# Attention with a bias: q and k of the last six pairs transposed by the DMA engines, and a new emission model

## The chip, the cores and the metric

The kernel runs on one core of a Trainium2 chip. The metric is device time in microseconds (us) of one execution. Before the change the median of 3 runs is 238.55 us (238.26 to 239.92). TensorE multiplies matrices (PE in the profile; PEld is its weight load), ScalarE evaluates functions (ACT), VectorE works elementwise (DVE), GpSimd (POOL) and SyncE (SP) here mostly issue DMAs. Each engine runs its own instructions in order; semaphores hold them until their inputs are there.

## The reference

Inputs: q, k and v of 4 batches x 8 heads x 1024 positions x 64, and one bias of 1024 x 1024 for all heads, float32.

```python
scale = 1.0 / np.sqrt(head_dim)
scores = scale * np.matmul(q, k.transpose(0, 1, 3, 2))
scores = scores + bias
scores_max = np.max(scores, axis=-1, keepdims=True)
attn = np.exp(scores - scores_max) / (np.sum(np.exp(scores - scores_max), axis=-1, keepdims=True) + 1e-8)
return np.matmul(attn, v).astype(np.float32)
```

## The kernel before

**Slots.** The 32 heads are 16 pairs, in groups of 4, 6 and 6 pairs (`GROUPS`). A query chunk has 128 rows, 8 chunks to a head. One chunk of one head is a slot, 256 in all. A slot is filled by 8 matmuls of 128x128x128 into one of three places in PSUM (`places`, of two banks each; `fill_half`, L221 and L224). Its 128x1024 scores are exponentiated into an `E` tile (`exp`, L238, on ScalarE; ring of 9), and 8 matmuls with V and a column of ones (`av`, L291) write 65 columns of a bank `po`. After 3 to 7 slots the bank is evicted by VectorE (`evac`, L299 reciprocal and L301 product) into one of two `ob` buffers, and SP stores it.

**Bias by difference.** A place's scores aren't cleared between heads: the bias is added by TensorE only at the first slot of a run (L221). After that each score matmul adds the next head's scores and takes off the ones before: `ko` and `qo` hold, on the 128 partitions, both heads of a pair (64 and 64), with the first head's q negated; `ke` and `qe` hold the first head of the pair and the second head of the pair before, negated. `qs` and `qz` hold one head with zeros beside it, for the starts.

**Preparation of a pair.** POOL loads k and q (L134, L142; `land` has 3 buffers each) and V, cast to bf16. VectorE lays the two heads side by side (`side_by_side`, L149, into `kr` and `qr`, two buffers each). TensorE transposes 128x128 blocks into a PSUM tile `px` (`transposes`, L178), which takes one of the two tags that the `po` banks also use. VectorE copies it out into `ko` (L185) or `qo` (L187, with the sign); and halves of these are doubled into `ke` (L196, or by an SP copy from pair 4 on, L495) and `qe`, `qs`, `qz` (L198, on VectorE or POOL). `kq` is a ring of 9 pairs.

**Slots on VectorE.** Some slots of the third place (19 in this version) are exponentiated by VectorE instead of ScalarE, in six steps on 128x1024 (`d_steps`: L255 dy, L260 df, L264 dt, L267 df, L270 dt, L275 de). L255 frees the PSUM place; the rest can wait.

**Order.** After a written-out prologue, a planner in the kernel's source (from T0 on) emits the order of each engine's instructions. It holds costs in ns, dates at which loads land (`land_at`, `v_at`, `bias_at`) and dates at which arrays are `ready`, and picks the next piece of work: for VectorE by `dve_pick` (earliest start, then a priority), for SP by date from `sp_q`. A slot goes to VectorE when `may_d` allows it and `backlog` is under `ROOM`. The planner's dates order the program; what an engine waits for on the chip is set by the semaphores alone.

Of the kernel before, what the change touches and what calls it, by code (L numbers as in the profile page):

```python
# [9 lines left out]
BF = mybir.dt.bfloat16  # L10
ACTF = mybir.ActivationFunctionType
ALU = mybir.AluOpType
# [4 lines left out]
def kernel(  # L17
# [13 lines left out]
    nc = tc.nc  # L31
    B, H, S, D = q.shape
    P = 128
# [10 lines left out]

    GROUPS = (4, 6, 6)
    RING = 9
    NE = 9
    C0 = 3

# [111 lines left out]
    def arrays(pr):  # L161
        if pr not in arrs:
            t = {x: kq.tile([P, NCH, P], BF, name=x) for x in (("ko", "ke", "qo", "qe") if pr else ("ko", "qo"))}
            if pr in split_pair:
                t["qs"] = qs
            if pr in first_pair:
                t["qz"] = qz[group_of[pr] % 2]
            arrs[pr] = t
        return arrs[pr]

    def linked(pr):
        return pr + 1 < NP

# [25 lines left out]
                            op0=ALU.mult, op1=ALU.mult)  # L199

    def parts(pr, which):
        return ([0] if pr else []) + ([1] if linked(pr) else []) + (
            [] if which else [2] * (pr in split_pair) + [3] * (pr in first_pair))

    def operands(s):
# [108 lines left out]
    with tc.manual_schedule():  # L314
# [60 lines left out]
        for c in range(5, NCH):  # L375
# [5 lines left out]
        EXP = 906  # L381
        ISSUE, COPY = 70, 4000
        T0 = 7400.0
        bias_at = {0: T0, 1: 8300, 2: 9700, 3: 20800, 4: 25600, 5: 30500, 6: 32000, 7: 33500}
        land_at = {(1, 1, 0): 11300, (1, 0, 0): 12100, (2, 1, 0): 15200, (2, 0, 0): 15800, (3, 1, 0): 18700,
                   (3, 0, 0): 19300, (0, 0, C0): 21700, (3, 0, C0): 24200, (1, 0, C0): 26600, (2, 0, C0): 27600}
        v_at, vland_at = {}, {0: 13600, 1: 17200, 2: 23200, 3: 29200}
        t_dma = 33500
# [6 lines left out]
        raw_at = {}  # L395

        q_items = [(p, 0, 0, C0) for p in range(1, GROUPS[0])] + [(p, 0, C0, NCH - C0) for p in (0, 3, 1, 2)]
        q_items += [(p, 0, 0, NCH) for p in range(GROUPS[0], NP)]
        k_items = [(p, 1, 0, NCH) for p in range(1, NP)]
        n1 = GROUPS[0] - 1  # L400
        pieces = [y for x in zip(k_items[:n1], q_items[:n1]) for y in x] + q_items[n1:n1 + GROUPS[0]]
        pieces += [y for x in zip(k_items[n1:], q_items[n1 + GROUPS[0]:]) for y in x]
# [11 lines left out]
        half_done = []  # L414
        waiting, free_lands, loads = [], set(), list(range(GROUPS[0], NP))
        sp_q, t_sp = [], T0
        AHEAD = 60
        DEP = 115
        ROOM = 5000
# [15 lines left out]
        def arrange(pr, which, c0, n):  # L435

            if (pr, which, c0) not in land_at:
                waiting.append((pr, which, c0, n))
                return
            urgent = need_at[pr, which, c0] - next_fill < 12  # L440
            cost = 90 + 40 * n

            def run(t2):
                side_by_side(pr, which, slice(c0, c0 + n))
                raw_at[pr, which, c0] = t2 + cost + L_DVE
                if which == 0 and c0 + n == NCH:
                    free_lands.add(pr)
                    while loads and loads[0] - 3 in free_lands:
                        load(loads.pop(0), t2)
            dve_q.append((land_at[pr, which, c0], 0 if urgent else 2, cost, run))  # L450

        def load(pr, t):
            load_k(pr)
            load_q(pr, slice(0, NCH))
            land_at[pr, 1, 0] = dma(pool(t, 750), 1800)
            land_at[pr, 0, 0] = dma(pool(t, 750), 1800)
            for p in [pr - 1] * (pr > GROUPS[0]) + [pr] * (pr + 1 == NP):
                load_v(p)
                v_at[p] = dma(pool(0, 1900), 4800)
            for x in [x for x in waiting if x[0] == pr]:  # L460
                waiting.remove(x)
                arrange(*x)

        def move_v(pr):
            def run(t2):
# [4 lines left out]
        def dma(at, cost):  # L470

            nonlocal t_dma
            t_dma = max(t_dma, at) + cost
            return t_dma + 2500

        def doubles(pr, which, c0, n, t2, urgent):
            for x in parts(pr, which):
                key = (("ke", "ke1")[x], pr + (x == 1)) if which else (("qe", "qe1", "qs", "qz")[x], pr + (x == 1), c0)
                if which and pr >= GROUPS[0]:
                    sp_q.append((t2 + L_DVE, lambda t3, x=x, key=key: copy_k(pr, x, key, t3)))  # L480
                elif which or urgent:
                    cost = 90 + 38 * n

                    def run(t3, x=x, key=key, cost=cost):
                        double(pr, which, c0, n, x, nc.vector)
                        ready[key] = t3 + cost + L_DVE
                    dve_q.append((t2, 0.2 if urgent else 2, cost, run))
                else:
                    double(pr, which, c0, n, x, nc.gpsimd)
                    pool(t2)  # L490
                    ready[key] = pool(0, 125 * n + 100) + 300
# [38 lines left out]
        def pe_cands():  # L530

            out = []
            for x in range(3):
                if not queue[x] or queue[x][0] > next_fill + WINDOW:
                    continue
                s = queue[x][0]
                r = fill_ready(s)
                if r is not None and (before[s] is None or before[s] in used):
                    cost = FILL * (2 if slots[s][3] else 1)

                    def do(t, s=s, x=x, cost=cost):
                        nonlocal next_fill
                        fill(s)
                        filled[s] = t + cost + L_PE
                        queue[x].pop(0)
                        next_fill = min([y[0] for y in queue.values() if y], default=NS)
                        if may_d[s] and backlog(t) < ROOM:
                            dslots.add(s)
                            avq.remove(s)
                            start_d(s)  # L550
                        else:
                            acts.append(s)
                    out.append((max(t_pe, r), cost, do, 0, s))
# [36 lines left out]
            if pieces:  # L590
# [39 lines left out]
        def pool(at, cost=0):  # L630
            nonlocal t_pool
            t_pool = max(t_pool, at) + cost
            return t_pool
# [8 lines left out]
                x_free[tag] = t2 + cost + L_DVE  # L642
            dve_q.append((t, 1, cost, run))

        chains, d_wait = [], []

        def backlog(t):
            x = max(0, t_dve - t) + sum(y[2] for y in dve_q if y[0] < t + 3000 and y[1] < 3)
            return x + sum(sum(y[0] for y in c) for c in chains) / 2 + sum(sum(y[0] for y in c[1:]) for r, s, c in d_wait) / 2

        def start_d(s):
            steps = d_steps(s)

            def first(t):
# [12 lines left out]
        def step(s, left, t):  # L667
            cost = left[0][0]

            def run(t2):  # L670
                left.pop(0)[1]()
                if left:
                    step(s, left, t2 + cost + DEP)
                    return
                dav.append((t2 + cost + L_DVE, s))
                chains[:] = [x for x in chains if x is not left]
                next_chain(t2 + cost)
            dve_q.append((t, 3, cost, run))

        def pe_pick():  # L680
            c = pe_cands()
# [13 lines left out]
            return min(ok + fills, key=lambda x: (x[0], x[3])) if ok + fills else None  # L695

        def dve_pick():
            if not dve_q:
# [12 lines left out]
        for x in k_items[:2] + q_items[:2]:  # L711
            arrange(*x)
        while next_fill < NS or next_act < len(acts) or avq or dav or dve_q or sp_q:
            c = []
# [65 lines left out]
```

## Time and profile before

| | value |
|---|---|
| median of 3 runs | 238.55 us |
| the profiled execution | 238.78 us |
| its span | 237.0 us |
| granted TensorE clock | 0.996 |
| DMA | 27.37 MB, mean 115 GB/s |
| exponentials on ScalarE | 236 full and 2 halves: 237 slots |
| slots on VectorE | 19 |

A row of the groups gives line, engine, operation, result and operands by name, shape, count, then busy us, mean ns of one, and idle us of the engine just before them with what ended it. Instructions overlap a little, so that a mean is longer than the step from one start to the next (an exponential takes 1084 ns on the mean, and ScalarE takes one each 0.92 us). A row of a timeline gives start, length, engine, line, operation, count and the gap ahead of it.

### The profile page before, as it was taken

The page shows a single profiled execution, that of the slowest core. Times are in us where ns is not written, and L with a number is a line of the kernel's source. Part 1 is how long each engine was busy: PE and PEld are TensorE (multiplying, and loading weights), DVE is VectorE, ACT ScalarE, POOL GpSimd, SP SyncE. Part 2 cuts the span into 40 slices and gives each one's busy share as a digit, 9 for nine tenths or more (in the row PEclk, how much of TensorE's full clock was granted, in tenths as well). Part 3 has the DMA queues.
Part 4 walks back from the last instruction along what each step waited for, and adds up shares of the span by engine and source line. Part 5 has one row for each costly group of instructions (what it writes and reads, how often), then busy time and mean ns, then how long its engine had stood idle before and what let it go on. Part 6 is the DMA issues. An engine that isn't in the chain of part 4 may idle for free.

```text
span 237.0 us, 10333 instructions
## 1 busy us (share of the span) xinstructions
PE 222.2 (94%) x4554; PEld 212.3 (90%) x4554; DVE 209.2 (88%) x335; ACT 222.0 (94%) x242; POOL 59.0 (25%) x80
## 2 busy tenths in 40 slices
PE   7779999999999999999999997999999999999883
PEld 2668999999999998999999996999999999999873
DVE  2668855799999989999999999999999999999981
ACT  3589999989999999999999999899999999999993
POOL 8828283710185414400000176000000000000000
PEclk9999999999999999999999999999999999999998
DMA  6999999992399999992111769133321111121112
GB/s 204 208 203 189 209 221 193 201 185 70 73 152 217 221 218 206 165 94 75 35 28 42 148 85 168 40 76 86 95 65 42 42 39 33 36 64 42 30 42 79
DMA packets 56140, 27.37 MB, mean 115 GB/s; under 512 B 32864, under 2 KB 53600, under 8 KB 56096
## 3 DMA queue, kind: packets, MB, share of 16 engines
q0 software_dynamic: 36304, 14.06, 50.2%
q1 hardware_dynamic: 19648, 12.13, 19.0%
q8 instruction: 35, 0.57, 1.0%
q10 hardware_dynamic: 144, 0.52, 0.7%
q14 instruction: 9, 0.07, 0.1%
HBM read 29.36 MB, written 8.39 MB: 159 GB/s over the span
## 4 chain that ended last, share of the span: by engine, by line
PE 54%; ACT 20%; DVE 15%; issue 7%; DMA 2%; SPq 0%; ACTq 0%; DVEq 0%
PE pl L224 30%; ACT E L238 20%; PE po L291 16%; PE px L178 5%; PE pl L221 4%; DVE ko L185 2%; DMA dt<-in_k_dram 2%; DVE qe L198 2%; DVE dt L270 1%; DVE qo L187 1%; DVE dt L264 1%; DVE ob L301 1%; DVE ke L196 1%; DVE dy L255 1%; DVE kr L149 1%
## 5 line engine op out<-in xcount | busy, mean ns | idle before, releaser
L238 ACT ACTIVATE E<-pl 128x1024 bf16<-128x1024 f32 (+1 forms) x238 | 218.8, 1084 | 6.6 <-PE pl L224 5.8
L291 PE MATMUL po<-vall,E 128*128 128x65 bf16 x1896 | 89.5, 194 | 1.5 <-issue 0.7
L224 PE MATMUL pl<-qo,ko 128*128 128x128 bf16 x1024 | 77.2, 219 | 4.0 <-ACT E L238 1.9
L224 PEld LDWEIGHTS <-ko 128*128 128x128 bf16 x1216 | 73.2, 98 | 7.0 <-issue 4.7
L291 PEld LDWEIGHTS <-E 128*128 128x128 bf16 x1896 | 76.5, 98 | 2.4 <-issue 1.2
L224 PE MATMUL pl<-qe,ke 128*128 128x128 bf16 x832 | 61.7, 219 | 2.5 <-DVE qe L198 1.2
L224 PEld LDWEIGHTS <-ke 128*128 128x128 bf16 x832 | 50.2, 98 | 4.8 <-issue 2.3
L134 POOL DMA_DIRECT2D k<-in_k_dram x15 | 11.2, 748 | 62.9 <-DVE kr L149 62.9
L255 DVE TENSOR_SCALAR dy<-pl 128x1024 int32<-128x1024 f32 x19 | 23.2, 1219 | 3.0 <-ACT E L238 2.6
L301 DVE TENSOR_TENSOR ob<-po,rs 128x384 f32<-128x384 f32 (+4 forms) x44 | 24.0, 546 | 1.5
L267 DVE SCALAR_TENSOR_TENSOR df<-dt,df 128x1024 f32<-128x1024 f32 x19 | 23.9, 1260 | 0.0
L275 DVE SCALAR_TENSOR_TENSOR de<-dy,dt 128x1024 uint16<-128x1024 int32 x19 | 23.3, 1229 | 0.0
L264 DVE SCALAR_TENSOR_TENSOR dt<-df 128x1024 f32<-128x1024 f32 x19 | 23.1, 1217 | 0.1
L270 DVE SCALAR_TENSOR_TENSOR dt<-df,dt 128x1024 f32<-128x1024 f32 x19 | 23.1, 1217 | 0.0
L159 POOL DMA_DIRECT2D vall<-in_v_dram x24 | 21.0, 878 | 0.4 <-issue 0.4
L142 POOL DMA_DIRECT2D q<-in_q_dram x18 | 13.0, 725 | 16.8 <-DVE qr L149 16.6
L221 PE MATMUL pl<-ident,braw 128*128 128x128 bf16 x192 | 16.1, 227 | 0.0
L187 DVE TENSOR_SCALAR qo<-px,sgn 128x1024 bf16<-128x1024 bf16 (+2 forms) x20 | 12.8, 639 | 2.4 <-PE px L178 2.4
L185 DVE COPY ko<-px 128x1024 bf16<-128x1024 bf16 (+1 forms) x17 | 11.1, 653 | 4.2 <-PE px L178 4.2
L198 DVE TENSOR_SCALAR qe<-qo 64x1024 bf16<-64x1024 bf16 (+2 forms) x35 | 13.8, 395 | 0.9
L299 DVE RECIPROCAL rs<-po 128x6 f32<-128x6 f32 (+4 forms) x44 | 8.4, 191 | 6.8 <-PE po L291 6.4
L221 PEld LDWEIGHTS <-braw 128*128 128x128 bf16 x192 | 14.0, 148 | 0.0
(48 smaller groups left out, 127.5 us busy)
## 6 DMA issues: line engine op xcount, KB each, us to landing
out_dram<-ob SPq DMA_DIRECT2D x52, 96.0 KB, 3.0
k<-in_k_dram POOLq DMA_DIRECT2D x15, 256.0 KB, 7.0
q<-in_q_dram POOLq DMA_DIRECT2D x12, 256.0 KB, 6.9
vall<-in_v_dram POOLq DMA_DIRECT2D x24, 128.0 KB, 7.1
ke<-ko SPq DMA_DIRECT2D x23, 128.0 KB, 4.7
out_dram<-ob SPq DMA_DIRECT2D x34, 64.0 KB, 1.9
braw<-in_bias_dram POOLq DMA_DIRECT2D x7, 256.0 KB, 6.9
v<-in_v_dram POOLq DMA_DIRECT2D x4, 256.0 KB, 6.4
```

Of the source, the lines that this page charges most:

```text
L159: nc.gpsimd.dma_start(out=vall[:, 2 * pr + t, :, :D], in_=vf[pr, :, t])
L198: w.tensor_scalar(to[("qe", "qe", "qs", "qz")[part]][rows, cs, :], t["qo"][rows, cs, :], -1.0, 1.0, op0=ALU.mult, op1=ALU.mult)
L221: nc.tensor.matmul(to, braw[:, c, :].rearrange("p (kp kc) -> p kc kp", kc=NCH)[:, kc, :], ident8[:], start=i == 0, stop=False, skip_group_ ...
L224: nc.tensor.matmul(to, kk[:, kc, :], qq[:, c, :], start=False, stop=True, skip_group_check=True)
L238: nc.scalar.activation(e[:, i:i + n].rearrange("p b x -> p (b x)"), places[slots[s][0]][:, i:i + n].rearrange("p b x -> p (b x)"), ACTF.Ex ...
L255: w.tensor_scalar(t["y"][:], places[slots[s][0]].rearrange("p b x -> p (b x)"), scale * LOG2E * 65536.0, 127.0 * 65536.0, op0=ALU.mult, op ...
L264: w.scalar_tensor_tensor(t["t"][:], t["f"][:], -G, t["f"][:], op0=ALU.add, op1=ALU.mult)
L267: w.scalar_tensor_tensor(t["f"][:], t["t"][:], Q, t["f"][:], op0=ALU.mult, op1=ALU.add)
L270: w.scalar_tensor_tensor(t["t"][:], t["f"][:], V, t["t"][:], op0=ALU.add, op1=ALU.mult)
L275: w.scalar_tensor_tensor(etile[s].bitcast(U16).rearrange("p c q -> p (c q)"), t["y"][:], 1.0 / 512.0, t["t"][:], op0=ALU.mult, op1=ALU.add)
L291: nc.tensor.matmul(po[:, j, :], etile[s][:, kc, :], vall[:, h, kc, :], start=j == 0 and kc == 0, stop=kc == NCH - 1, skip_group_check=True)
L301: nc.vector.tensor_tensor(ob[:, :n, :], po[:, :n, :D], rs[:, :n, :].to_broadcast([P, n, D]), op=ALU.mult)
```

## The change

`TURNED = 10`: pairs 10 to 15 (the last group) take another way from the loaded array to `ko`, `qo`, `ke` and `qe`. For k VectorE makes the same copy as before (L185 in the changed file); for q it makes four half copies (L186 to L189), which are two laid-out arrays: one with the first head negated (for `qo`), one with the second head of the pair before, negated (for `qe`). SP then issues DMAs that transpose the eight 128x128 blocks of each array straight into `ko`, `qo` and `qe` (L193): three for each pair, 18 in all. `ke` is copied on SP as before, `qz` (pair 10) and `qs` (pair 14) are copied on SP from `qe`. For these pairs TensorE's transposes, the copy-out and the doublings are gone, and so is the doubling from pair 9 into pair 10's `qe`.

The planner's dates and rules change too: bias, loads and V are booked earlier by 0.2 to 2.0 us; a doubling of its own pair comes ahead of the one for the next pair; at most three slots of VectorE may be open; their last step waits while two finished ones are in stock; ScalarE takes the smallest slot number among those already filled; TensorE transposes ahead of need only while fewer than four finished exponentials wait for their product with V, instead of six. The order that results holds 20 slots on VectorE.

```diff
+    TURNED = 10
...
+    def layout_steps(pr, which):
+        l = lands[pr, which]
+        t = {}
...
+        if which:
+            return [(410, lambda: nc.vector.tensor_copy(new(0).rearrange("p c t d -> p t c d"), l[:]))]
+        minus = lambda to, of: nc.vector.tensor_scalar(to, of, -1.0, None, op0=ALU.mult)
+        return [(HALF, lambda: minus(new(0)[:, :, 0, :], l[:, 0])),
+                (HALF, lambda: nc.vector.tensor_copy(t[0][:, :, 1, :], l[:, 1])),
+                (HALF, lambda: nc.vector.tensor_copy(new(1)[:, :, 0, :], l[:, 0])),
+                (HALF, lambda: minus(t[1][:, :, 1, :], lands[pr - 1, 0][:, 1]))]
+
+    def turn(to, of):
+        nc.sync.dma_start_transpose(to[:], of.rearrange("p c t d -> p c (t d)"))
...
     def parts(pr, which):
-        return ([0] if pr else []) + ([1] if linked(pr) else []) + (
+        return ([0] if pr else []) + ([1] if linked(pr) and (which or pr + 1 < TURNED) else []) + (
...
-        bias_at = {0: T0, 1: 8300, 2: 9700, 3: 20800, 4: 25600, 5: 30500, 6: 32000, 7: 33500}
+        bias_at = {0: T0, 1: max(T0, 8100), 2: 9300, 3: 19400, 4: 24000, 5: 28700, 6: 30300, 7: 31900}
...
-        q_items += [(p, 0, 0, NCH) for p in range(GROUPS[0], NP)]
-        k_items = [(p, 1, 0, NCH) for p in range(1, NP)]
+        q_items += [(p, 0, 0, NCH) for p in range(GROUPS[0], TURNED)]
+        k_items = [(p, 1, 0, NCH) for p in range(1, TURNED)]
...
+        def turning(to, of, t):
+            nonlocal t_turn, t_sp
+            turn(to, of)
+            t_sp += 1230
+            t_turn = max(t_turn, t) + 2700
+            return t_turn + 2200
+
+        def turn_k(pr, t):
+            done = turned[pr, 1] = ready["ko", pr] = turning(arrays(pr)["ko"], raws[pr, 1, 0], t)
+            for x in (0, 1)[:NP - pr]:
+                sp_q.append((done, lambda t2, x=x: copy_k(pr, x, (("ke", "ke1")[x], pr + x), t2)))
+
+        def turn_q(pr, t):
+            a = arrays(pr)
+            ready["qo", pr, 0] = turning(a["qo"], raws[pr, 0, 0], t)
+            done = turned[pr, 0] = ready["qe", pr, 0] = ready["qe1", pr, 0] = turning(a["qe"], raws[pr, 0, 1], t)
+            for x in ("qs", "qz"):
+                if x in a:
+                    def copy(t2, x=x):
+                        nc.sync.dma_start(out=a[x][:D], in_=a["qe"][:D])
+                        ready[x, pr, 0] = t2 + COPY
+                    sp_q.append((done, copy))
...
-            t_dma = max(t_dma, at) + cost
-            return t_dma + 2500
+            t_dma = max(t_dma + cost, at + 4700)
+            return t_dma + 200
...
-                    dve_q.append((t2, 0.2 if urgent else 2, cost, run))
+                    dve_q.append((t2, (0.2, 0.4, 0.4, 0.2)[x] if urgent else 2, cost, run))
...
-                        if may_d[s] and backlog(t) < ROOM:
+                        if may_d[s] and backlog(t) < ROOM and len(open_d) < 3:
...
-                        and (lag < 6 or need - next_fill < 8 or half_done)):
+                        and (lag < 4 or need - next_fill < 8 or half_done)):
...
-            dve_q.append((t, 3, cost, run))
+            dve_q.append((t, 3 if len(left) > 1 else 4, cost, run))
...
-            best = min(dve_q, key=lambda x: (max(x[0], t_dve), x[1]))
+            best = min(can, key=lambda x: (max(x[0], t_dve), x[1]))
...
-                s = acts[next_act]
+                s = min(x for x in acts[next_act:] if filled[x] <= max(t_act, filled[acts[next_act]]))
```

A new function of the planner, `advance`, decides when a pair's layout and transposition begin: not before its loads are booked as landed, at most 60 slots ahead of its first use, and after the pair before is booked as transposed.

More of the change, by code (lines that the diff above doesn't have):

```diff
@@ L169, in arrays, with new @@
         return arrs[pr]
+    HALF = 205
+    def layout_steps(pr, which):
+        l = lands[pr, which]
+        t = {}
+        def new(x):
+            raws[pr, which, x] = t[x] = raw.tile([P, NCH, 2, D], BF, name="qk"[which] + "r")
+            return t[x]
+        if which:
[7 more added lines that the diff above has]
+        nc.sync.dma_start_transpose(to[:], of.rearrange("p c t d -> p c (t d)"))
     def linked(pr):
@@ L383 @@
         T0 = 7400.0
-        bias_at = {0: T0, 1: 8300, 2: 9700, 3: 20800, 4: 25600, 5: 30500, 6: 32000, 7: 33500}
[L385 to L388, printed above, removed]
+        bias_at = {0: T0, 1: max(T0, 8100), 2: 9300, 3: 19400, 4: 24000, 5: 28700, 6: 30300, 7: 31900}
+        land_at = {(1, 1, 0): 10500, (1, 0, 0): 11100, (2, 1, 0): 13700, (2, 0, 0): 14300, (3, 1, 0): 17700,
+                   (3, 0, 0): 18000, (0, 0, C0): 20200, (3, 0, C0): 22300, (1, 0, C0): 24800, (2, 0, C0): 25600}
+        v_at, vland_at = {}, {0: 12500, 1: 15600, 2: 21400, 3: 27400}
+        t_dma = 31900
         t_pe, t_act, t_dve, t_pool = T0, T0, T0, T0 + 20000
@@ L416 @@
         sp_q, t_sp = [], T0
+        turns, turned, t_turn = [(p, x) for p in range(TURNED, NP) for x in (1, 0)], {}, T0
         AHEAD = 60
@@ L445, in run @@
                 raw_at[pr, which, c0] = t2 + cost + L_DVE
-                if which == 0 and c0 + n == NCH:
+                if which == 0 and c0 + n == NCH and pr + 1 < TURNED:
                     free_lands.add(pr)
@@ L454, in load @@
             load_q(pr, slice(0, NCH))
-            land_at[pr, 1, 0] = dma(pool(t, 750), 1800)
-            land_at[pr, 0, 0] = dma(pool(t, 750), 1800)
+            land_at[pr, 1, 0] = dma(pool(t, 750), 1400)
+            land_at[pr, 0, 0] = dma(pool(t, 750), 1400)
             for p in [pr - 1] * (pr > GROUPS[0]) + [pr] * (pr + 1 == NP):
                 load_v(p)
-                v_at[p] = dma(pool(0, 1900), 4800)
+                v_at[p] = dma(pool(0, 1900), 2400)
             for x in [x for x in waiting if x[0] == pr]:
@@ L462, in load, with advance, run @@
                 arrange(*x)
+        def advance():
+            while turns:
+                pr, which = turns[0]
+                ring = pr + 1 - RING
+                if ((pr, which, 0) not in land_at or next_fill < first_slot[pr] - AHEAD or last_slot[ring] >= next_fill
+                        or any(y[1] == which for y in pieces) or pr > TURNED and (pr - 1, which) not in turned
+                        or which == 0 and pr in split_pair and any(
+                            x[3] and x[2] // 2 in split_pair and x[2] // 2 < pr for x in slots[next_fill:])):
+                    return
+                turns.pop(0)
+                prio = 0 if first_slot[pr] - next_fill < 12 else 2
+                steps = layout_steps(pr, which)
+                left = list(steps)
+                def run(t, pr=pr, which=which, left=left, prio=prio):
+                    cost, step = left.pop(0)
+                    step()
+                    if left:
+                        dve_q.append((t + cost, prio, cost, run))
+                        return
+                    if which == 0:
+                        free_lands.add(pr - 1)
+                        while loads and loads[0] - 3 in free_lands:
+                            load(loads.pop(0), t)
+                    sp_q.append((t + cost + L_DVE, lambda t2: turn_k(pr, t2) if which else turn_q(pr, t2)))
+                dve_q.append((max(land_at[pr, which, 0], turned.get((pr - 1, which), 0)), prio, steps[0][0], run))
@@ L643, in close @@
             dve_q.append((t, 1, cost, run))
-        chains, d_wait = [], []
+        chains, d_wait, open_d = [], [], set()
         def backlog(t):
@@ L652, in start_d @@
             steps = d_steps(s)
+            open_d.add(s)
             def first(t):
@@ L675, in run @@
                 dav.append((t2 + cost + L_DVE, s))
+                dav.sort()
+                open_d.discard(s)
                 chains[:] = [x for x in chains if x is not left]
                 next_chain(t2 + cost)
-            dve_q.append((t, 3, cost, run))
+            dve_q.append((t, 3 if len(left) > 1 else 4, cost, run))
         def pe_pick():
@@ L697, in dve_pick @@
         def dve_pick():
-            if not dve_q:
+            can = [x for x in dve_q if x[1] < 4 or len(dav) < 2]
+            if not can:
                 return None
-            best = min(dve_q, key=lambda x: (max(x[0], t_dve), x[1]))
+            best = min(can, key=lambda x: (max(x[0], t_dve), x[1]))
             start = max(best[0], t_dve)
@@ L713 @@
         while next_fill < NS or next_act < len(acts) or avq or dav or dve_q or sp_q:
+            advance()
             c = []
             if next_act < len(acts):
-                s = acts[next_act]
+                s = min(x for x in acts[next_act:] if filled[x] <= max(t_act, filled[acts[next_act]]))
+                acts.remove(s)
+                acts.insert(next_act, s)
                 if next_act < NE or acts[next_act - NE] in av_done:
```

## The prediction

> **What bounds the kernel now.** I read four views: the page's busy times, ScalarE's timeline, the groups with shapes kept apart, and the DMA rows. First the busy times: three engines are near full, so one has to be picked.
>
> ```profile
> PE 222.2 (94%) x4554; PEld 212.3 (90%) x4554; DVE 209.2 (88%) x335; ACT 222.0 (94%) x242; POOL 59.0 (25%) x80
> ```
>
> TensorE's 222 us overstates it: matmuls overlap. By the steps between starts (0.45 us per 8 score matmuls, 0.26 per 8 of L291, 0.50 per 8 of bias, 0.46 per 8 transposes), 256 slots need 182 us, the bias 12, the transposes 14.7: 208 us in the 223 us that ScalarE's exponentials last. So it has 15 us in hand. ScalarE's timeline (start, length, gap before and its releaser) shows that ScalarE has almost nothing in hand:
>
> ```profile
> 9.38 5.67 ACT L238 ACTIVATE E<-pl 128x512 bf16<-128x512 f32 x7 [1.95 <-PE pl L224]
> 15.93 18.79 ACT L238 ACTIVATE E<-pl 128x1024 bf16<-128x1024 f32 x20 [0.89 <-PE pl L224]
> 35.27 12.94 ACT L238 ACTIVATE E<-pl 128x1024 bf16<-128x1024 f32 x14 [0.55 <-PE po L291]
> 48.55 1.02 ACT L238 ACTIVATE E<-pl 128x1024 bf16<-128x1024 f32 x1 [0.34 <-PE pl L224]
> 49.95 31.45 ACT L238 ACTIVATE E<-pl 128x1024 bf16<-128x1024 f32 x34 [0.37 <-PE pl L224]
> 81.98 23.04 ACT L238 ACTIVATE E<-pl 128x1024 bf16<-128x1024 f32 x25 [0.58 <-PE pl L224]
> 105.29 42.45 ACT L238 ACTIVATE E<-pl 128x1024 bf16<-128x1024 f32 x46 [0.27 <-PE pl L224]
> 148.82 51.48 ACT L238 ACTIVATE E<-pl 128x1024 bf16<-128x1024 f32 x56 [1.08 <-PE pl L224]
> 200.65 32.25 ACT L238 ACTIVATE E<-pl 128x1024 bf16<-128x1024 f32 x35 [0.35 <-PE pl L224]
> ```
>
> From the first exponential at 9.38 to the end of the last at 232.90 lie 223.5 us; 218.8 are busy (the page's L238 row), 4.4 are the eight gaps shown and 0.3 smaller ones. The span is 9.4 of prologue, 218.8 of exponentials, 4.7 of gaps, 4.1 of tail: 237.0. Time can leave through fewer exponentials on ScalarE or through the gaps, and no other way while prologue and tail stay as they are.
>
> **The change, part by part.** Sums are against the profiled execution, 238.78 us (span 237.0 and 1.78 around it); the median of the runs is 238.55, 0.23 lower, and I put the forecast on that.
>
> *One slot more on VectorE.* The changed program holds 20 starts of the six-step chain instead of 19, and 236 slots on ScalarE instead of 237. 218.8 / 238 = 0.92 us leave ScalarE. VectorE pays six steps: 1219, 684, 1217, 1217, 1260 and 1229 ns, 6.8 us.
>
> *Group 3's preparation leaves TensorE and VectorE.* The groups by shape (busy us, mean ns | idle before):
>
> ```profile
> L267 DVE SCALAR_TENSOR_TENSOR df<-dt,df 128x1024 f32<-128x1024 f32 x19 | 23.9, 1260 | 0.0
> L260 DVE TENSOR_SCALAR df<-dy 128x1024 f32<-128x1024 uint16 x19 | 12.9, 684 | 0.0
> L185 DVE COPY ko<-px 128x1024 bf16<-128x1024 bf16 x15 | 10.2, 683 | 3.5 <-PE px L178 3.5
> L198 DVE TENSOR_SCALAR qe<-qo 64x1024 bf16<-64x1024 bf16 x21 | 9.4, 447 | 0.5
> L187 DVE TENSOR_SCALAR qo<-px,sgn 128x1024 bf16<-128x1024 bf16 x12 | 8.9, 745 | 0.0
> L149 DVE COPY qr<-q 128x1024 bf16<-128x1024 bf16 x12 | 5.0, 420 | 0.3 <-PE px L178 0.3
> L149 DVE COPY qr<-q 128x640 bf16<-128x640 bf16 x3 | 0.9, 316 | 0.0
> L149 DVE COPY qr<-q 128x384 bf16<-128x384 bf16 x3 | 0.8, 261 | 0.2 <-DMA q<-in_q_dram 0.2
> ```
>
> For six pairs VectorE loses L185 (6 x 683), L187 (6 x 745), the qr copy (6 x 420) and ten qe doublings and one qs (11 x 447): 16.0 us. POOL loses two qe and the qz, 4.0 us. VectorE gains 24 half copies of 128x512; between the 384 and 640 rows that is 0.29 us each, 6.9 us. The k copy stays. Net: 16.0 - 6.9 = 9.1 saved, 6.8 spent on the extra slot, 2.3 us less. TensorE loses 12 x 8 transposes, 5.5 us. Neither is on ScalarE's path by itself; they pay only where a gap comes from them.
>
> *Which gaps go.* The 1.08 gap before 148.82 is preparation: TensorE's next score fill waited 1.61 us for L255 (dy) on VectorE, which was late behind these two rows of VectorE's timeline, both while POOL doubled qe and qz:
>
> ```profile
> 141.83 1.22 DVE L149 COPY kr<-k 128x1024 bf16<-128x1024 bf16 x1
> 144.94 2.05 DVE L267 SCALAR_TENSOR_TENSOR df<-dt,df 128x1024 f32<-128x1024 f32 x1
> ```
>
> They took 0.8 more than their groups' usual 0.42 and 1.22. There the changed program has no copy-out, no doubling and no POOL work on qe; I take the gap as gone. The 0.89 gap at 15.04 is pair 1: TensorE waits for qe (L198), made behind ko, ke, qo, ke. Now q1's transposes precede the third place's fill, and the second ke comes after qe: one copy step, 0.45 us, earlier. The other gaps, where the bias adds 0.5 us a fill (31 to 50) or an order was unlucky, stay: I grant them 0.3, as the planner's new landings are earlier. Gaps: 4.7 - 1.08 - 0.45 - 0.3 = 2.9.
>
> *What is added: 18 transposing DMAs on SP and two plain copies.* The trace holds none, so I bound their duration from both sides. These are the hardware queue's row (packets, MB, share of 16 engines' span), and of the existing ke copies the issue on SP and the time to landing:
>
> ```profile
> q1 hardware_dynamic: 19648, 12.13, 19.0%
> L495 SPq DMA_DIRECT2D ke<-ko x23: 467/542/1592, 59.5 to 170.3; - x23
> DMA to landing us min/median/max: 2.2/4.7/7.4
> ```
>
> A packet there costs 0.19 x 16 x 237 us / 19648 = 36.7 ns. An array is 1024 rows of 256 bytes; as 256-byte packets, 64 per engine, it takes 2.35 us; cut into 32-byte pieces, 18.8 us. I take 2.35, since source and result both lie in 256-byte rows, plus 2.2 to land, and keep both ends. On SP an issue costs 0.5 to 1.6 us, at most 29 for 18; SP waited 95 us for ob alone, so that is covered. A DMA can't take less than nothing, so no gain lies here.
>
> Queued behind them: on VectorE, the first q layout of the next pair writes a qr buffer (two per pair, two in the pool) that the pair before is still being transposed from; on SP, the ke copies wait for ko to land, and output stores stand behind. By the changed order, some ten VectorE instructions (1.13 us per long step) lie between a pair's last layout and the next pair's first, about 10 us; two q transposes need 1.1 + 2 x 2.35 + 2.2 = 8.0. SP is held by a ke copy for about 1.1 x 3 + 2.35 = 5.7 us against an eviction every 5.2 (44 in 223 us) and two ob buffers. Both fit, with little over. Readers are far off: q of pair 10 is laid out at fill 98 and needed at 160, pair 15's at 169 and needed at 190; at 0.87 us a slot, 54 and 18 us.
>
> The Trainium skill has two rules here. "DMA: Bandwidth & Descriptors", section "Latency and other measured facts", gives 261 GB/s for a DMA transpose with a non-contiguous middle dimension; by it an array takes an estimated 1.0 us, and nothing above changes. "VectorE: DVE Perf Modes", section "The three transpose paths", gives 390 ns for a 128x128 block on TensorE and 1309 ns by DMA, and says to use TensorE where a PSUM result will do; by it the eight blocks of an array take an estimated 10.5 us one after another, and the rival below decides. No transposing DMA in this trace settles it.
>
> **Sum.** 9.4 + (218.8 - 0.9) + 2.9 + 4.1 = 234.3 span, + 1.8 = 236.1, - 0.23 = 235.8. Own range 234.3 (1.5 us less gap) to 236.9 (the 1.08 gap stays).
>
> **The rivals.** *Only the slot pays, or the saving is eaten* (0.25). Gaps move instead of going: 238.55 - 0.92 = 237.6. Beside that, POOL's loads may slow the half copies as at 141.83: POOL is busy about 16% of 98 to 172 us; 24 x 0.8 x 0.16 = 3.1 us turns the 2.3 saved into 0.8 lost, about 238.5 to 239. For it: VectorE is 93 to 99% busy in each 10 us from 50 to 230. Against: preparation's share of it shrinks.
>
> *Transposes too slow for their buffers* (0.20). Place: VectorE's L186 and L189 in `layout_steps`, waiting for the transposes of the pair before; everything on VectorE stands behind, the dy step that frees TensorE's third place among it, then ScalarE. It decides from (10 - 1.1 - 2.2) / 2 = 3.4 us an array. With 128-byte pieces, 4.7 us: 1.1 + 9.4 + 2.2 - 10 = 2.7 us, four times (pairs 11, 13, 14, 15; pair 12 has some 17 us), 11 us, less the 2.8 won: 247. With 64-byte pieces, 9.4 us: 12 x 4 = 48, about 284. For it: no row excludes it. Against: landings of 128 KB copies in 4.7. In it, 0.03 that it isn't a block transpose at all (32-byte pieces or less), beyond 300.
>
> **How the numbers follow.** The forecast has 0.55: 235.8. About 1% is what a measurement of this kernel can tell from no change: 236.16 to 240.94. Of the forecast's own range four fifths lie below 236.16: faster 0.45. The rest of it and the first rival: same 0.35. Slower 0.20. The range runs from 234.0, a little below the own range, over the first rival to 241.5, where transposes only just miss (two windows short by 1.5 us): about 0.03 is left out below, 0.16 above.
>
> **What would show it.** Right: L238 x237 with about 217.9 us busy; gaps on ScalarE near 3 us, none near 148; half copies near 0.29 us; transposes landing in under 6 us; VectorE's busy time near 207. Wrong: idle on VectorE before L186 or L189 released by a DMA, or before L325 (ob) by a store; TensorE waiting for ko, ke or qe on a DMA; half copies near 0.6; a new gap of over 1 us on ScalarE.

## The result, and the profile after

| | before | after |
|---|---|---|
| median, side by side on the same chips | 239.04 us (4 runs) | 254.88 us (4 runs, 254.06 to 257.5) |
| ratio | | 1.068, 95% interval 1.0588 to 1.0772 |
| profiled execution, span | 238.78, 237.0 us | 257.5, 255.4 us |
| granted TensorE clock | 0.996 | 0.982 |

The kernel became 6.8% slower. Medians are of all executions; ratios and intervals, here and below, leave out executions more than 1.5% above the fastest of the same kernel. In the changed file the exponential is L262, the score matmuls L248, the product with V L315, the eviction L323 and L325, the half copies L186 to L189 and the transposing DMA L193. First the busy times of the page after:

```profile
PE 221.8 (87%) x4458; PEld 210.4 (82%) x4458; DVE 204.8 (80%) x336; ACT 223.5 (88%) x241; POOL 54.8 (21%) x77
```

But for 1.5 us on ScalarE none of the engines in this row has more to do than before (VectorE 4.4 us less); all of them stand still more. ScalarE's timeline shows where (start, length, operation, count, then the gap ahead and its releaser):

```profile
86.13 24.86 ACT L262 ACTIVATE E<-pl 128x1024 bf16<-128x1024 f32 x27 [0.31 <-PE pl L248]
112.13 1.98 ACT L262 ACTIVATE E<-pl 128x1024 bf16<-128x1024 f32 x2 [1.15 <-PE pl L248]
...
121.40 1.94 ACT L262 ACTIVATE E<-pl 128x1024 bf16<-128x1024 f32 x2 [1.77 <-PE pl L248]
...
135.16 16.61 ACT L262 ACTIVATE E<-pl 128x1024 bf16<-128x1024 f32 x18 [2.20 <-PE pl L248]
153.18 3.77 ACT L262 ACTIVATE E<-pl 128x1024 bf16<-128x1024 f32 x4 [1.42 <-PE pl L248]
159.49 1.94 ACT L262 ACTIVATE E<-pl 128x1024 bf16<-128x1024 f32 x2 [2.54 <-PE pl L248]
...
175.85 1.02 ACT L262 ACTIVATE E<-pl 128x1024 bf16<-128x1024 f32 x1 [4.81 <-PE pl L248]
177.14 1.02 ACT L262 ACTIVATE E<-pl 128x1024 bf16<-128x1024 f32 x1 [0.27 <-PE pl L248]
179.04 72.12 ACT L262 ACTIVATE E<-pl 128x1024 bf16<-128x1024 f32 x78 [0.88 <-PE pl L248]
```

The sum in the prediction's form is 9.32 to the first exponential + 220.4 of exponentials + 21.4 of gaps + 4.2 of tail = 255.4 (before: 9.4 + 218.8 + 4.7 + 4.1). The gaps from 112 to 179 us, those left out included, hold 17.8 us; in the same stretch before there was the one of 1.08. After 179.04, when the last q layout is done, nothing stalls any more. The rows also show part of why the exponentials take 220.4 us with one slot fewer: a stretch of n lasts about 0.92 n + 0.10 (1.02, 1.94), and 24 stretches instead of 9 cost an estimated 15 x 0.10 = 1.5 us.

ScalarE names only TensorE's fills. What is behind most of them stands in VectorE's waits (for what, total us, times, longest):

```profile
DVE qr L189 <- DMA qe<-qr: 10.3, 2, 6.3
DVE ob L325 <- DMA out_dram<-ob: 9.4, 4, 5.9
...
DVE qr L186 <- DMA qo<-qr: 0.6, 1, 0.6
```

These are the three waits that the prediction named as signs of its being wrong: 20.3 us in which VectorE stood, with the dy steps that free the third place behind it. The rows of the transposing DMA (count, ns on SP min/median/max; last, us from issue to landing):

```profile
L193 SPq DMA_TRANSPOSE ko<-kr x6: 1242/1622/2957, 99.3 to 174.6; - x6
L193 SPq DMA_TRANSPOSE qo<-qr x6: 1231/1329/1466, 101.2 to 182.1; - x6
L193 SPq DMA_TRANSPOSE qe<-qr x6: 1279/3954/4302, 102.5 to 183.6; - x6
...
DMA to landing us min/median/max: 3.1/7.5/13.7
```

The least is what a transpose takes with nothing beside it (pair 15's q, after 182 us: 3.2 to 3.3); for pairs 10 to 13 it is 6.1 to 13.7, but for one of 4.1. POOL's timeline says what stands beside those:

```profile
136.57 0.71 POOL L143 DMA_DIRECT2D q<-in_q_dram  x1 [18.32 <-DVE rs L323]
137.28 1.91 POOL L160 DMA_DIRECT2D vall<-in_v_dram  x2
139.18 0.72 POOL L135 DMA_DIRECT2D k<-in_k_dram  x1
153.25 0.71 POOL L143 DMA_DIRECT2D q<-in_q_dram  x1 [13.35 <-DVE qr L186]
153.95 3.54 POOL L160 DMA_DIRECT2D vall<-in_v_dram  x4
```

A pair's last q layout frees a `land` buffer, so POOL starts the next loads in the very moment in which SP starts that pair's transposes (137.6 and 139.1; 154.4 and 155.7). The queue rows of the page give nearly the cost of a packet that the prediction had, and much work on both queues:

```profile
q0 software_dynamic: 36304, 14.06, 49.9%
q1 hardware_dynamic: 39104, 17.12, 36.6%
```

0.366 x 16 x 255.4 / 39104 = 38.2 ns a packet. Against the row before, q1 has 19456 packets and 4.99 MB more, 256 bytes each, so that the transposes do move in pieces of 256 bytes. The Trainium skill, "DMA: Bandwidth & Descriptors", section "Queues, rings and completion order", says that a DMA engine takes the queues that have work in turn, packet by packet; the trace fits this in that the same 256 KB lands in 3.2 us alone and in up to 13.7 beside loads, but it does not show the turns themselves.

Last, one stall as VectorE saw it, and SP's timeline of the same time:

```profile
145.42 0.20 DVE L323 RECIPROCAL rs<-po 128x7 f32<-128x7 f32 x1
151.52 0.62 DVE L325 TENSOR_TENSOR ob<-po,rs 128x448 f32<-128x448 f32 x1 [5.90 <-DMA out_dram<-ob]
```

```profile
135.19 2.34 SPq L193 DMA_TRANSPOSE ko<-kr  x1
137.63 1.40 SPq L193 DMA_TRANSPOSE qo<-qr  x1
139.12 4.05 SPq L193 DMA_TRANSPOSE qe<-qr  x1
143.26 1.54 SPq L718 DMA_DIRECT2D out_dram<-ob  x3
```

Evictions at 136.41 and 139.98 filled both `ob` buffers; their stores could be issued only at 143.26, behind 7.8 us of transposes on SP, and then landed in up to 7.7 us (3.1 is the median of the large stores). The third eviction waited until 151.5.

### The profile page after: what moved, and what is told of

Read it like the earlier page. It is cut to its first block, busy times and chain, and to the rows that moved or that the text cites. A ratio compares the mean times of both kernels' runs of the same rounds, so it can differ in the third digit from the quotient of the medians.

```text
span 255.4 us, 10216 instructions
## 1 busy us (share of the span) xinstructions
PE 221.8 (87%) x4458; PEld 210.4 (82%) x4458; DVE 204.8 (80%) x336; ACT 223.5 (88%) x241; POOL 54.8 (21%) x77
## 3 DMA queue, kind: packets, MB, share of 16 engines
q1 hardware_dynamic: 39104, 17.12, 36.6%
## 4 chain that ended last, share of the span: by engine, by line
PE 42%; DVE 19%; DMA 17%; ACT 13%; issue 5%; SPq 2%; DVEq 0%; ACTq 0%
PE pl L248 24%; ACT E L262 13%; PE po L315 12%; DMA out_dram<-ob 9%; DMA qe<-qr 5%; PE pl L245 3%; PE px L202 3%; DVE dt L294 3%; DMA dt<-in_k_dram 2%; DVE ob L325 2%; DVE dy L279 2%; SPq L718 2%; DVE ko L209 1%; DVE df L291 1%; DVE dt L288 1%
## 5 line engine op out<-in xcount | busy, mean ns | idle before, releaser
L262 ACT ACTIVATE E<-pl 128x1024 bf16<-128x1024 f32 (+1 forms) x237 | 220.4, 1066 | 23.1 <-PE pl L248 21.8
L315 PE MATMUL po<-vall,E 128*128 128x65 bf16 x1888 | 93.6, 195 | 7.6 <-issue 3.5
L315 PEld LDWEIGHTS <-E 128*128 128x128 bf16 x1888 | 79.0, 99 | 9.0 <-issue 4.0
L248 PE MATMUL pl<-qo,ko 128*128 128x128 bf16 x1024 | 78.9, 221 | 4.7 <-DVE dy L279 2.2
L248 PEld LDWEIGHTS <-ko 128*128 128x128 bf16 x1216 | 74.9, 99 | 8.4 <-issue 4.9
L248 PE MATMUL pl<-qe,ke 128*128 128x128 bf16 x832 | 63.1, 219 | 5.8 <-DVE dy L279 4.0
L248 PEld LDWEIGHTS <-ke 128*128 128x128 bf16 x832 | 50.9, 98 | 8.8 <-issue 4.7
L325 DVE TENSOR_TENSOR ob<-po,rs 128x384 f32<-128x384 f32 (+4 forms) x44 | 24.0, 546 | 10.8 <-DMA out_dram<-ob 9.4
L288 DVE SCALAR_TENSOR_TENSOR dt<-df 128x1024 f32<-128x1024 f32 x20 | 24.4, 1218 | 0.0
L323 DVE RECIPROCAL rs<-po 128x6 f32<-128x6 f32 (+4 forms) x44 | 8.4, 192 | 10.9 <-PE po L315 10.7
L135 POOL DMA_DIRECT2D k<-in_k_dram x15 | 10.7, 714 | 22.3 <-DVE kr L150 20.3
L315 PE MATMUL po<-vall,de 128*128 128x65 bf16 x160 | 8.5, 195 | 6.3 <-DVE de L299 6.3
L284 DVE TENSOR_SCALAR df<-dy 128x1024 f32<-128x1024 uint16 x20 | 13.6, 685 | 0.0
L315 PEld LDWEIGHTS <-de 128*128 128x128 bf16 x160 | 6.5, 98 | 6.5 <-DVE de L299 6.5
```

Source lines behind the costliest of these rows:

```text
L248: nc.tensor.matmul(to, kk[:, kc, :], qq[:, c, :], start=False, stop=True, skip_group_check=True)
L262: nc.scalar.activation(e[:, i:i + n].rearrange("p b x -> p (b x)"), places[slots[s][0]][:, i:i + n].rearrange("p b x -> p (b x)"), ACTF.Ex ...
L284: w.tensor_scalar(t["f"][:], t["lo"], G / 65536.0, None, op0=ALU.mult)
L288: w.scalar_tensor_tensor(t["t"][:], t["f"][:], -G, t["f"][:], op0=ALU.add, op1=ALU.mult)
L315: nc.tensor.matmul(po[:, j, :], etile[s][:, kc, :], vall[:, h, kc, :], start=j == 0 and kc == 0, stop=kc == NCH - 1, skip_group_check=True)
L325: nc.vector.tensor_tensor(ob[:, :n, :], po[:, :n, :D], rs[:, :n, :].to_broadcast([P, n, D]), op=ALU.mult)
```

## The experiments

Theory A: the transposes hold VectorE through the two `qr` and two `ob` buffers. B: the planner's new rules and order cost the time. C: the DMA engines are full of all the traffic. D: the transposes are slow only beside the loads that the same layout releases. Ratios are against the kernel before, on the same chips.

**Planner's rules alone.** Nothing is turned by DMA, 19 slots are on VectorE.

```diff
-    TURNED = 10
+    TURNED = 16
```

> TURNED = 16: no pair is transposed by DMA, all other changes of the planner stay. Theory A (the transposing DMAs hold VectorE through the two ob buffers and the two qr buffers): without them the stalls go, 236 to 240 us, no gap over 1.5 us on ScalarE after 100 us. Rival B (the planner's new rules make the bad order): stays above 248 us. Rival C (the DMA engines are full): like A, 236 to 240 us.

240.19 us, 1.0055 (1.0022 to 1.0088). The rules bring nothing, they cost half a per cent, and they are not the loss either. ScalarE's timeline shows the first gap down from 0.89 to 0.15 and new ones instead:

```profile
14.87 18.73 ACT L262 ACTIVATE E<-pl 128x1024 bf16<-128x1024 f32 x20 [0.15 <-PE pl L248]
...
76.06 6.70 ACT L262 ACTIVATE E<-pl 128x1024 bf16<-128x1024 f32 x7 [0.52 <-PE pl L248]
83.41 1.94 ACT L262 ACTIVATE E<-pl 128x1024 bf16<-128x1024 f32 x2 [0.65 <-PE pl L248]
...
99.55 52.53 ACT L262 ACTIVATE E<-pl 128x1024 bf16<-128x1024 f32 x57 [1.47 <-PE pl L248]
152.35 24.86 ACT L262 ACTIVATE E<-pl 128x1024 bf16<-128x1024 f32 x27 [0.27 <-PE pl L248]
```

Behind the last of the new gaps, at 99.55, stands a stop of TensorE for which the profile shows no wait (`issue`); there is one of 0.76 us before the gap at 83.41 too:

```profile
98.61 0.40 PE L315 MATMUL po<-vall,E 128*128 128x65 bf16 x7 [1.25 <-issue]
```

**The two buffer sets.** One array ring fewer (`kq` 8) makes room; the order of the instructions is the changed kernel's. The control has only the smaller ring.

```diff
-    raw = ctx.enter_context(tc.tile_pool(name="raw", bufs=2))
-    kq = ctx.enter_context(tc.tile_pool(name="kq", bufs=RING))
+    raw, rawq = (ctx.enter_context(tc.tile_pool(name=x, bufs=2)) for x in ("raw", "rawq"))
+    kq = ctx.enter_context(tc.tile_pool(name="kq", bufs=RING - 1))
...
-    op = ctx.enter_context(tc.tile_pool(name="op", bufs=2))
+    op = ctx.enter_context(tc.tile_pool(name="op", bufs=4))
...
-            raws[pr, which, x] = t[x] = raw.tile([P, NCH, 2, D], BF, name="qk"[which] + "r")
+            raws[pr, which, x] = t[x] = (rawq if pr % 2 and not which else raw).tile([P, NCH, 2, D], BF, name="qk"[which] + "r")
```

> Control: only the kq buffer that the runs with more ob and qr buffers gave up (8 instead of 9), same order of instructions. Every theory: 253 to 257 us, as the changed kernel.

> Four ob buffers instead of two (and one kq buffer less to make room), same order of instructions on every engine. Theory A: VectorE's 9.4 us of waiting for stores go, its wait for qr stays: 245 to 249 us. Rival B: 253 to 256. Rival C (full DMA engines; the wait moves to another place, ke or ko): 253 to 256 with TensorE waiting for ke or ko.

> Four qr buffers for the turned pairs instead of two (and one kq buffer less), same order of instructions. Theory A: VectorE's 10.9 us of waiting for the transposes go, its 9.4 us for the stores stay or grow: 244 to 250 us. Rivals B and C: 253 to 256.

> Four ob and four qr buffers (and one kq buffer less), same order of instructions. Theory A: both waits go, 236 to 240 us, at or below the kernel before. Rival B: above 250. Rival C: above 248, TensorE waiting for ke, ko or qe, or VectorE for loads.

| kernel | median us | ratio (interval) | VectorE's waits for qr; for ob |
|---|---|---|---|
| changed | 254.88 | 1.068 (1.0588 to 1.0772) | 10.9; 9.4 |
| control, `kq` 8 | 251.46 | 1.0522 (1.0479 to 1.0565) | 5.9; 7.5 |
| 4 ob | 248.70 | 1.0375 (1.0293 to 1.0458) | 6.1, and 4.1 for a load; 0 |
| 4 qr | 250.09 | 1.0435 (1.036 to 1.0511) | 0; 16.2 |
| both | 242.61 | 1.0142 (1.0078 to 1.0206) | 0; 0 |

Freed alone, each set leaves its wait with the other, as VectorE's waits show, first with 4 ob, then with 4 qr (whose profiled execution took 253.77 us, more than its median):

```profile
DVE qr L189 <- DMA qe<-qr: 5.2, 3, 2.0
DVE qr L186 <- DMA vall<-in_v_dram: 4.1, 1, 4.1
```

```profile
DVE ob L325 <- DMA out_dram<-ob: 16.2, 5, 7.9
```

Both together take back 12.3 us of the changed kernel's 15.8 and 8.9 of the control's, which is the fairer comparison; the transposes land no sooner (median 8.4 us). That is theory A, though the time is 2.6 us above what it expected. C as stated is out: the same 39104 packets pass in a span of 239.9 us, and of TensorE's waits for ke, ko and qe by DMA only one of 0.7 us is left. Why the control itself is 3.4 us below the changed kernel was not pursued; its two waits are 13.4 us against 20.3. In the version with both, ScalarE stops at 112, 120 and 127 us, 3.6 us in all with two small gaps beside them, and in one stretch of 115 exponentials after 130 not at all. TensorE's timeline there:

```profile
111.45 0.42 PE L315 MATMUL po<-vall,E 128*128 128x65 bf16 x8 [1.75 <-issue]
118.74 0.42 PE L315 MATMUL po<-vall,E 128*128 128x65 bf16 x8 [1.42 <-issue]
126.31 0.61 PE L248 MATMUL pl<-qz,ko 128*128 128x128 bf16 x8 [0.88 <-issue]
```

The profile shows nothing that TensorE waits for. The DMAs that bring instructions, 16 KB each and otherwise mostly 4 to 7 us apart, came 7.4 to 9.3 us apart here (starting at 98.4, 107.7, 116.2 and 123.6), and the three stops end 3.8, 2.5 and 2.7 us after the start of one. The same holds for the two stops with nothing turned (loads at 82.1 and 96.1, stops that end 2.8 and 2.5 us later), so that such stops don't need the transposes. Against it as a proof: before the change two of these loads lie 10.0 us apart (65.3, 75.4) with no such stop.

**The loads moved behind the transposes.** POOL copies one element of `qe` first, so that the loads released by a turned pair's q layout start when its transposes have landed.

```diff
+            if held:
+                nc.gpsimd.tensor_copy(gate[:], a["qe"][:, 0, 0:1])
+            for f in held:
+                f()
+            held.clear()
```

With the changed kernel's buffers and order; with the four ob and four qr buffers; the same with a planner that books the loads from the landing on; and with both buffer sets again, only V held.

> POOL copies one element of qe before it issues the loads that the last q layout releases, so that these loads start only when the pair's transposes have landed; same buffers, same order of instructions on the other engines. Theory D (the transposes are slow only beside the loads that the same layout step lets go): all transposes land within 5 us, VectorE waits under 3 us in sum for ob and qr, 237 to 242 us. Theory A without D (a transpose is slow by itself, only buffers help): landings stay at 6 to 13 us, 250 to 256 us.

> The same with four ob and four qr buffers (and one kq buffer less). Theory D: little more than the loads alone bring, 236 to 239 us, and TensorE's gaps without a visible cause near 110 to 127 us, which I take for late instruction loads in the crowd, shrink below 1 us each. If these gaps have another cause, they stay and the time is 240 to 243.

> Four ob and four qr buffers, and the loads that a turned pair's q layout releases are issued only after that pair's transposes have landed (POOL copies one element of qe first), as before; but now the planner knows it and books the loads from the landing on, so that the order of VectorE no longer expects them early. Theory D: transposes land in 3 to 6 us, no wait of VectorE for the k load of pair 15 (9.8 us in the run in which the planner did not know), TensorE has no idle over 0.8 us put down to issue from 100 to 130 us: 237.5 to 240.5. If the loads simply come too late in this scheme (each pair's loads wait for two transposes and then take 7 to 9 us): the waits for k return, 243 to 248.

> The kernel with four ob and four qr buffers (1.0142), with only the V loads that a turned pair's q layout releases held back until that pair's transposes have landed (POOL copies one element of qe first); k and q loads are released as before, and the order on the other four engines is the same. Theory D (the crowd of loads and transposes delays the instruction loads, which costs TensorE about 4 us at 110 to 127 us): with half of the crowd's bytes moved later, the landings of transposes fall by some 2 us, the three issue gaps of TensorE (1.75, 1.42, 0.88) shrink to under half, and the time is 238.5 to 241. Rival: the gaps have another cause (the order itself): they stay, 242 to 243.5. Against both: V then comes late for its products, a wait of TensorE for vall, 243 or more.

| kernel | median us | ratio (interval) | landing of transposes, median |
|---|---|---|---|
| loads held | 246.97 | 1.0328 (1.0283 to 1.0374) | 5.0 to 6.2 by kind |
| held, both buffer sets | 249.19 | 1.0425 (1.0375 to 1.0476) | 5.9 to 6.8 by kind |
| held and planned, both sets | 245.28 | 1.0251 (1.0192 to 1.031) | 5.9 |
| V held, both sets | 242.48 | 1.0108 (1.007 to 1.0146) | 6.3 |

Holding the loads helps the changed kernel by 7.9 us, with waits for qr and ob down from 20.3 to 4.3 us: theory D, in part. Pairs 10 and 12, with at most the end of the loads beside them, now land in 3.1 to 5.2 us; those of pairs 11, 13 and 14 that meet the held loads of the pair before still take 6.4 to 9.2. And what is held comes late: VectorE waits 6.1 us for k in this run. Its waits with both sets, first held, then with the planner told:

```profile
DVE kr L186 <- DMA k<-in_k_dram: 12.2, 2, 9.8
```

```profile
DVE kr L186 <- DMA k<-in_k_dram: 7.8, 1, 7.8
```

A late k takes the place of the two old waits (L186 is the k copy in these two files). In the first of the two, none of TensorE's three stops of 110 to 127 us is left; with V alone held, two of the three are gone and this one stays:

```profile
124.48 0.61 PE L249 MATMUL pl<-qz,ko 128*128 128x128 bf16 x8 [1.03 <-issue]
```

So with the order unchanged the stops move when the loads move, which speaks for delayed instruction loads; but 1.0108 against 1.0142 is no gain that the intervals bear out (in its profiled execution, 244.8 us, VectorE waited 4.1 us for a ko transpose).

**Plain copies in place of transposes.** The same bytes in the same 256-byte pieces; the transposition is left out, so that `ko`, `qo` and `qe` hold the rows as laid out.

```diff
-        nc.sync.dma_start_transpose(to[:], of.rearrange("p c t d -> p c (t d)"))
+        [nc.sync.dma_start(out=to[:, i::2], in_=of.rearrange("p c t d -> p c (t d)")[:, i::2]) for i in range(2)]
```

> Each transposing DMA becomes two plain DMAs of every other 128x128 block (same bytes, same 256-byte pieces): the transposition itself is left out. If the pieces beside the loads are the cause and not the transposition: landings of 6 to 12 us beside the loads, VectorE waits 10 us or more, 248 to 256 us. If the transposing mode is what is slow: landings under 5 us, 237 to 241 us.

246.57 us, 1.0318 (1.0259 to 1.0377). The rows of the copies:

```profile
L193 SPq DMA_DIRECT2D qe<-qr x12: 593/674/1843, 102.1 to 173.3; - x12
...
DMA to landing us min/median/max: 2.3/5.4/9.7
```

VectorE still waits 4.2 us for qr and 5.6 for ob. By the medians, 7.5 of the 15.8 us come with moving these bytes at that time by any DMA; the other 8.3 with the transposing form, whose issue holds SP for up to 4.3 us (the two plain ones of an array up to 3.3) and whose landing takes up to 13.7. So both rivals of this run are right in part.

**Fewer pairs.** Only the last two or the last four pairs are turned; the last two also with the booked dates and rules of the kernel before. `TURNED` is 14 as shown for the last two and 12 for the last four. The other line of the edit makes the planner begin at most one layout at each call.

```diff
-    TURNED = 10
+    TURNED = 14
...
-            while turns:
+            if turns:
```

> Only pairs 14 and 15 are turned by DMA (six transposes instead of 18); pairs 10 to 13 go through TensorE again; planner rules, 20 slots on VectorE, two ob and two qr buffers as in the changed kernel. In this order no load of POOL is released by the layout of a turned pair. Theory D (transposes are slow only beside the loads that the same layout releases): transposes land in 3 to 5 us, VectorE waits for a DMA at qr or ob for less than 1 us in all, DMA slices are far from full after 100 us, and the time is that of the planner's rules alone (240.2) less the slot (0.9): 238.5 to 240.5. Theory A without D (transposes hold the two qr buffers whatever else runs): pair 15's q layout waits about 4 us and a store about 2, 243 to 246. Theory C (the engines are full from all the traffic of 100 to 178 us): as D here, since two thirds of the added packets are gone.

> Pairs 12 to 15 are turned by DMA (twelve transposes); the rest as in the changed kernel. Here the q layouts of pairs 12 and 13 release loads, those of 14 and 15 none: two crowds instead of the changed kernel's four. Theory D: half of the changed kernel's loss, 244 to 249, with the waits of VectorE at qr and ob, 6 to 11 us in all, in the stretch after the layouts of 12 and 13 alone. Theory C (all the traffic): likewise, but the waits spread over 14 and 15 too. If the price were per transpose: 12 of 18, two thirds of the loss, 249 to 251.

> As the run with the last two pairs alone, but with the emission rules and booked landings of the kernel before (20 slots on VectorE come out of it too). Theory B (the new planner rules cost about 1.3 us where they stand alone): 1 to 1.5 us less than the run with the new rules, 237 to 239, so at or a little below the kernel before, the gap of 0.89 us at 15 us back and the small gaps from 76 to 100 us gone. If the new rules cost nothing once pairs 14 and 15 are off TensorE: the two are equal within 0.3%.

Last two: 245.21 us (one execution at 241.66, three at 245.1 to 245.38), 1.0169 (1.0079 to 1.026). Last four: 256.69, 1.0696 (1.0624 to 1.0767). Last two with the old rules: 248.57, 1.0389 (1.0356 to 1.0422). The last two pairs, which have no loads beside them, land as D says, and VectorE waits for none of their DMAs. The landing row, TensorE's timeline and ScalarE's:

```profile
DMA to landing us min/median/max: 3.1/3.7/4.9
```

```profile
181.11 2.74 PE L248 MATMUL pl<-qe,ke 128*128 128x128 bf16 x24 [1.91 <-DMA ke<-ko]
183.64 1.06 PE L248 MATMUL pl<-qo,ko 128*128 128x128 bf16 x8
```

```profile
182.24 1.94 ACT L262 ACTIVATE E<-pl 128x1024 bf16<-128x1024 f32 x2 [3.53 <-PE pl L248]
```

The time expected of it was missed all the same: these transposes begin at 161 us, after the last pair that TensorE turns, and end close to their use, so that a fill waits for pair 15's `ke`, copied on SP behind two transposes. The wait is 1.91 us, but ScalarE's gap there is 3.53, because TensorE then runs at a granted clock of 0.50, from 179.8 to 186.6 us (the 24 matmuls above take 2.74 us, and 24 of the same kind 1.50 at full clock in the run with four pairs). ScalarE's gaps after 178 us, 4.9 us against 0.8 with nothing turned, are about the 4.0 us between the spans of these two runs. With four pairs turned it is both: 6.8 us of qr waits beside the loads and 2.5 us for `ke`, and the loss of the whole change with two thirds of its transposes. A price per transpose is ruled out by that. B's expectation that the old rules would be faster is missed too, though with another order come other waits: TensorE waits 2.5 us for `qe` and 4.8 for dy there.

**The limit of six.** Nothing turned, the new rules but for one.

```diff
-                        and (lag < 4 or need - next_fill < 8 or half_done)):
+                        and (lag < 6 or need - next_fill < 8 or half_done)):
```

> Nothing is turned by DMA; the planner's rules are the new ones except that TensorE transposes ahead of need while fewer than six finished exponentials wait for V, as in the kernel before (19 slots on VectorE). Theory B' (of the new rules it is the limit of four that costs the gaps of 3.2 us at 76 to 100 us): those gaps shrink to under 1.5 us, the first gap stays at 0.15, and the time is 237.0 to 238.7, at or below the kernel before. Rival: the other new rules or dates make them: they stay, 239.5 to 241.

242.69 us, 1.0126 (1.0065 to 1.0187), with gaps of 1.75, 1.35 and 1.45 us between 79 and 100: lifting this limit does not take the gaps away. But they are not the same gaps (TensorE waits 1.64 us for a `ke` copy before the first), and two of those without turning are stops without a visible wait, so whether a rule makes them, and which, stays open. No version tried is faster than the kernel before.

## Why the prediction was wrong

*What held.* ScalarE was the bound, and its sum still adds up. 20 slots are on VectorE. Its half copies take 0.29 us, and its busy time is 204.8 us, near the 207 that the sum gave. The first gap went, by more than foreseen (0.89 to 0.15; 0.45 was granted). A transpose without loads beside it lands in 3.1 to 4.9 us where the working had 2.35 + 2.2 = 4.55, its pieces are the 256 bytes that were assumed, and a packet costs 38.2 ns where it had 36.7.

*The step that failed* is the one that ended with "Both fit, with little over". "Two q transposes need 1.1 + 2 x 2.35 + 2.2 = 8.0" priced them as if nothing else ran on the DMA engines. In the trace after, pair 13's two take 9.7 and 16.5 us from the end of its layout (152.95) to the half copies that wait for them (162.65 and 169.47): the second is issued 2.8 us after the layout and takes 13.7 to land. What was overlooked was in the code: the same last layout that starts the transposes frees the buffer that POOL's next k, q and V wait for. SP's 5.7 us were likewise 7.8, since the `qe` transpose, issued right behind that of `qo`, holds SP for about 4 us ("0.5 to 1.6 us" was the bound), and the stores behind them land late too. So both windows, VectorE's and SP's, failed at once: 20.3 us of VectorE, and 8.9 to 12.3 us of the time by the run that frees both (against the control and against the changed kernel). Part of this is TensorE's clock: after the stops it is at half for 2 x 3.41 us in the changed kernel, and with both sets it stays at 1.00 from 100 to 180 us.

*The rival that came* is "Transposes too slow for their buffers" (0.20), at its place, L186 and L189, at pairs 11 and 14 rather than in all four windows. It set its price by the size of a piece; the pieces were 256 bytes, and the loss came about half with moving these pieces beside the loads at all and half with the transposing form. The half of it that waits for `ob` was judged in the step and not priced in the rival, so that its 247 is 8 us short; the range to 241.5 allowed for windows that only just miss. "VectorE: DVE Perf Modes" in the Trainium skill, section "Rules for kernel authors", advises TensorE for a 128x128 transpose where a result in PSUM will do. Here that advice was right. Its section "The three transpose paths" has 1309 ns a block by DMA, by which an array takes an estimated 10.5 us; that is not what happens alone (3.2 us) and is within what happens beside loads.

*Sizes.* The exponentials were to fall to 217.9 us and rose to 220.4, 1.5 of it by the stretches counted above; the rest was not traced. The other gaps were granted 0.3 less and gained: 1.48 us at 76 to 86 against 0.58 before (at 81.98). Whether the gap before 148.82 went can't be seen in the changed kernel, whose stops lie over it (1.42 and 2.54 us before 153.18 and 159.49). In the run without any turning 0.27 stands in its place, so that the planner's order is enough for it, and it says nothing for leaving TensorE's transposes out.

*What remains* with both buffer sets, 3.8 us, is about the planner's 1.4 (240.19 less 238.78) plus the 3.6 of ScalarE's stops at 112 to 127 us less 0.9 for the slot, an estimate: the planner's 1.4 has such stops in it as well. The cause of these stops is supported, not shown: no run took the instruction loads alone away.

## What to carry to other kernels

Before a transfer is put in place of engine work, look for what is released at the same moment as it: the event that starts the new DMA may also free the buffer that other loads wait for, and a landing time taken alone is then short, here by a factor of two to four. Check every ring that the new queue neighbours feed (here `qr` and, through SP, the two `ob`), and test them freed together, because one freed alone leaves the wait with the other. A later start of the loads, or fewer transfers, only moved the wait elsewhere here (to a late k, or to `ke`), also where the planner knew of it.

## What the runs showed of the hardware

The `qe` transpose, issued 1.4 to 1.6 us after that of `qo`, holds SP for 3.9 to 4.3 us beside the loads (pairs 10 to 13); the other transposes hold it for 1.2 to 3.0. Pair 15's, with nothing beside them, take 1.3 to 1.4.

After stalls TensorE ran slower for a while. Its timeline after one of 3.93 us:

```profile
174.39 0.51 PE L315 MATMUL po<-vall,de 128*128 128x65 bf16 x8 [3.93 <-DVE de L299]
174.71 1.04 PE L248 MATMUL pl<-qo,ko 128*128 128x128 bf16 x8
...
178.84 0.61 PE L248 MATMUL pl<-qe,ke 128*128 128x128 bf16 x8
```

The granted clock is 0.50 from 174.6 to 178.0 and from 120.0 to 123.3 us, in each case for 3.41 us, and 1.00 beside them. The Trainium skill, "TensorE: Matmul & The Clock Gate", Part 1, has the half-rate clock after an idle window of about 3.4 us. These traces differ in that the window need not be idle: in the 3.41 us ahead of each of these stretches TensorE was busy for 0.20 and for 1.35 us, with a longest stop of 1.84 in the second. In the 16 traces the clock changes on a grid of 3.41 us; from 12 us on, each of the 27 windows at full clock in which TensorE was busy for up to 0.45 of the time was followed by half clock, none of some 1000 with 0.55 or more was, and between them it went both ways. The stop of 1.61 us before the change left its window 0.53 busy, in between, and cost no clock; with the last two pairs turned, a window that was 0.54 busy did.
